# Down projection in 29 blocks that grow from three pairs to eight, each operand tile loaded once

## The chip, the cores and the metric

The kernel runs on one NeuronCore of a Trainium2 chip. The core has five engines that each work through their own queue in order: TensorE (PE, matrix products; its weight loads are listed as PEld), VectorE (DVE), ScalarE (ACT), GpSimd (POOL) and SyncE (SP), which here only issues transfers. Transfers run on 16 DMA engines. The metric is the device time of one execution in microseconds (us), the median of several runs.

## The reference

One layer of a decoder in float32 on 512 tokens of width 2048: RMS norm, one input projection that feeds three token mixers (dilated attention, a convolution module, banded attention with sinks), an output projection with a residual, then a second RMS norm and a gated feed-forward part. What matters here is the last line:

```python
x = x + mix @ w_out[l]
h2 = _rms_norm(x, norm2_g[l])
x = x + (jax.nn.silu(h2 @ w_gate[l]) * (h2 @ w_up[l])) @ w_down[l]
```

The inner width is 5632, that is 44 tiles of 128. The product with `w_down` is called Down; `h2 @ w_gate` and `h2 @ w_up` are called Wide.

## The kernel before, in words

Everything is held transposed: a tile has 128 channels on its partitions and the 512 tokens along it. To keep float32 accuracy on a TensorE that takes rounded operands (fp32r), a weight tile is split into a rounded part (hi, tile `wh`) and the rest (lo, `wl`).

**Seven products.** Wide and Down use a Strassen-Winograd scheme: each matrix is cut in 2 x 2, and seven products of sums of the quarters take the place of eight. The 44 feature tiles are thereby 22 *pairs* (`NP`), pair j being feature tiles j and j + 22; the 16 output tiles are eight pairs n and n + 8. For every pair j there are seven operand tiles, one for each product q, each [128, 512] fp32r (256 KB; first half rounded, second half the rest). Wide computes them, ScalarE and VectorE split them, and they are stored to DRAM (`od[j]`), in four pieces (`sums1` to `piece4`, lines 972 to 1007) whose work stretches over the nine products after the block's last one.

**Blocks.** The last part of the kernel is a loop over blocks (lines 1068 to 1106): 44 Wide blocks, then the Down blocks of the list `DOWN` (d0, d1, ...). A Down block is (n, first, end): it adds to output tiles n and n + 8 what the pairs from first to end - 1 give. Its width w is end - first. Every output pair gets several blocks; between them its two tiles y live in DRAM (`x2d`), are loaded ahead of a block (`load_y`, two transfers, issued in the fourth product of the block before) and stored after it (`store`, four transfers of half a tile). The last block of an output pair stores to the result `outT`.

A block runs the seven products in the order 5, 1, 7, 6, 2, 4, 3 (`ORDER`). For a Down block each product is w matmuls of 512 columns with the rounded weights (L912) and w of 256 columns with the rest (L915). Here d4.3 stands for the fourth product of block d4.

**Weights of a block.** Four tiles of raw weights ("11", "12", "21", "22", each 128 x 128w) are loaded by SP (L209). GpSimd makes the sums that the seven products need (L174), due by product: four products ahead of the block, s = 21 + 22; three ahead, 21 = 21 + 11 in place; at its first product, s = s + 11 in place; at its third, s = s + 12. In the order of the products the weights are s, 11, 21, s, 12, 22, s. Each is split two products ahead of its use (`SPLIT_AHEAD`): ScalarE casts it into PSUM (L226, tile `wn`) and into SBUF (L227, `wh`, three buffers), VectorE subtracts (L228, `wl`, three buffers). There is one buffer each for the raw tiles 11, 12 and 21, two for 22 and two for s; a load for the next block waits until the last split that reads its buffer is done. So the next block's 21, 22 and 11, which are loaded in that order, are issued when the split of the block's third weight is done.

**Evacuation.** After each product the result is added from PSUM on VectorE in the iteration that follows: nothing after the first (it is taken with the third), one reduction after the second (L921), four sums after the third, two after each of the others (L926, L927). After the fourth come three sums of y on GpSimd (L1048 to L1050).

**Operand tiles of Down.** They sit in a pool of 71 tiles of 256 KB. After product i of a block, the tiles of that product which later blocks do not need are given up, and those that the next block needs in addition are loaded (`load_act`, L1064), issued by SP one product later. SP's transfers are issued in the order in which the program names them: one that waits for its buffer or its data holds up all behind it.

**The list before.** 24 blocks, three for each output pair, every one 6, 7 or 8 pairs wide, with a window that slides by one pair a block and wraps:

```
d0..d7    0-6  0-7  1-8  2-9  3-10 4-11 5-12 6-13      (first-end, n = 0..7)
d8..d15   6-14 7-15 8-16 9-17 10-18 11-19 12-20 13-21
d16..d23  14-22 15-22 16-23 17-24 18-25 19-26 20-27 21-28
```

Pairs from 22 on mean 0 to 5 again: these are loaded a second time (28 pairs of seven tiles in all), and a block that wraps loads each of its raw weight tiles in two transfers. d0 needs 42 tiles; they are loaded during the last Wide block, each product's six after that product has been done there.

Of the kernel before, what the change touches and what calls it, by code (L numbers as in the profile page):

```python
# [9 lines left out]
F32 = mybir.dt.float32  # L10
# [5 lines left out]
P = 128  # L16
T = 512
# [7 lines left out]
NF = 44  # L25
# [39 lines left out]
NP = NF // 2  # L65


_A = [0, 0, 1, 2, 3, 4, 5, 6]
_B = [_A[n] + (6 if n == 0 else 7) for n in range(8)]
_C = [b + 8 for b in _B]  # L70
DOWN = [(n, *w) for ab in (zip(_A, _B), zip(_B, _C), zip(_C, [a + NP for a in _A])) for n, w in enumerate(ab)]

LAID = (5, 7, 6, 4, 3, 1, 2)

# [35 lines left out]
def kernel(ctx: ExitStack, tc: tile.TileContext, xT, wi, wo, wgu, wd, cst_in, outT):  # L110
    nc = tc.nc
# [21 lines left out]
    def bank(name, cols=T):  # L133
        return psum["banks"].tile([P, cols], F32, name=name, tag="b")
# [55 lines left out]

    def down_block(n, half, first, end):

        parts = [(first, min(end, NP)), (0, end - NP)] if first < NP else [(first - NP, end - NP)]
        return [bass.AP(tensor=wd.tensor, offset=wd.offset + (n * P * NF + half * NP + a) * P,
                        ap=[[NF * P, P], [1, (b - a) * P]]) for a, b in parts if b > a]

    for t, (n, first, end) in enumerate(DOWN):
        group(f"d{t}", t % 2, (end - first) * P, {f"{i + 1}{k + 1}": down_block(n + 8 * i, k, first, end)
# [3 lines left out]
    at = {"entry": 0, "split": 0, "use": 0}  # L202
# [159 lines left out]
    for k in range(KT):  # L362
# [9 lines left out]
        hi, lo = h_hl.pop(k)  # L372
# [14 lines left out]
    def project(name):  # L387
        b = bank(name)
        for half in range(2):
            wh, wl = next_unit()  # L390
            for kk in range(8):
                k = 8 * half + kk
                s = slice(kk * P, (kk + 1) * P)
                mm3(b, wh[:, s], wl[:, s], h_hi[k], h_lo[k], k == 0, k == KT - 1)
                if kk % 2 == 1:
                    ticks.tick()
        return b
# [356 lines left out]
    for name in PROJ[HEAD4:]:  # L754
        kind, what, j = name[0], name[1], name[2:]
# [3 lines left out]
        b = project(name)  # L759
# [19 lines left out]
    b = box = boxes = shared = None  # L779
# [13 lines left out]
    x2d = {n: tc.dram_tile([P, T], F32, name=f"x2d{n}") for n in range(KT)}  # L793
# [46 lines left out]
    for half in range(2):  # L840
        for i, n in enumerate(OUT_ORDER[half]):
            if half == 1 and i == 2:
                ticks.drain()
                b = None
                open_banks(banks=4, high=2)
            b = bank(f"o{half}_{n}")
# [36 lines left out]
    od = {p: tc.dram_tile([P, 7 * T], F32, name=f"od{p}") for p in range(NP)}  # L883
    evacs, extras = [], []
# [6 lines left out]
    def later(n, fn, *args, queue=evacs):  # L891
        while len(queue) <= n:
            queue.append([])
        queue[n].append((fn, *args))
# [118 lines left out]
    def load_y(t):  # L1013
        if t < len(DOWN):
            for n in (DOWN[t][0], DOWN[t][0] + 8):
                y[t, n] = slot(f"y{t}_{n}")
                nc.sync.dma_start(y[t, n], x2d[n])

    class Down(Block):


        def __init__(self, t):
            super().__init__(f"d{t}", t % 2)
            self.n = DOWN[t][0]
            self.out = outT if t >= 16 else x2d
            self.tail = t == len(DOWN) - 1
            self.y1, self.y2 = y.pop((t, self.n)), y.pop((t, self.n + 8))

# [29 lines left out]
    acts = {}  # L1058

    def load_act(q, pairs):  # L1060
        for j in pairs:
            acts[q, j] = slot(f"a{q}_{j}", F32R)
            at = LAID.index(q)
            nc.sync.dma_start(acts[q, j].bitcast(F32), od[j % NP][:, at * T:(at + 1) * T])  # L1064

    EARLY = 6
    blk = gate = None
    for g in range(2 * NP + len(DOWN)):
        t = g - 2 * NP
        if t < 0:  # L1070
            p, m = divmod(g, 2)
            blk = Wide(p, m, gate if m else None)
            gate = blk if m == 0 else None
        else:
            n, first, end = DOWN[t]
            blk = Down(t)
        early_w = []
        for i, q in enumerate(ORDER):
            sums_now()
            run(evacs)  # L1080
            w = next_unit()
            if g == 0 and i < 2:
                blk.multiply(q, w, [ops[q, j] for j in range(EARLY)], last=False)
                early_w.append((q, w))
                if i == 1:
                    for q, w in early_w:
                        blk.multiply(q, w, [ops[q, j] for j in range(EARLY, NJ)], EARLY)
                    norm2a()
            elif t < 0:
                blk.multiply(q, w, [ops[q, j] for j in range(NJ)])  # L1090
            else:
                blk.multiply(q, w, [acts[q, j] for j in range(first, end)])
            if g == 0 and i == 2:
                norm2b()

            if t == -1:
                for j in range(NJ):
                    ops.pop((q, j))
                later(1, load_act, q, range(*DOWN[0][1:]), queue=extras)
            elif 0 <= t < len(DOWN) - 1:  # L1100
                for j in range(first, DOWN[t + 1][1]):
                    acts.pop((q, j))
                later(1, load_act, q, range(end, DOWN[t + 1][2]), queue=extras)
            if t >= -1 and i == 3:
                load_y(t + 1)
            run(extras)
# [85 lines left out]
```

## Time and profile before

| | |
|---|---|
| median of 3 runs | 1939.97 us (1939.64 to 1940.5) |
| profiled execution | 1939.71 us, of which span from first to last instruction 1937.9 us |
| TensorE busy | 1906.1 us (98%) |
| VectorE, ScalarE, GpSimd busy | 1471.6, 1338.9, 995.0 us |
| DMA queue of SP | 317.51 MB, 48.0% of 16 engines over the span |
| operand tiles of Down (a<-od) | 196 transfers of 256 KB |
| first product of Down | starts at 1489.93 us of the span |
| last product of Down | ends at 1934.1 us |

All times in rows are microseconds from the start of the span unless marked ns. "Busy" counts the time in which an engine executes something; matmuls are pipelined, so the distance from one start to the next is the pace. In a row with a tile such as `w('22', 'd1')` the tile is the raw weight "22" of block d1. A bracket at the end of a row gives the idle time before it and what ended it. The clock is the share of full speed that TensorE was granted.

### The profile page before, as it was taken

How to read it: one execution, taken by the hardware profiler on the slowest of the kernel's cores; microseconds unless marked ns; L12 is line 12 of the kernel's file. 1: busy time of each engine (PE TensorE's matmuls, PEld its weight loads, DVE VectorE, ACT ScalarE, POOL GpSimd, SP SyncE). 2: the span in 40 equal slices, each digit the busy share in tenths (PEclk: the TensorE clock that was granted, in tenths of full speed). 3: DMA queues.
4: the chain of work that ended last, by engine and by line, in shares of the span. 5: the costliest groups of instructions: out<-in, count | busy, mean ns of one | idle time of the engine just before them, and what ended most of it. 6: DMA issues, size and time to landing. Idle time of an engine off the chain costs nothing.

```text
span 1937.9 us, 29292 instructions
## 1 busy us (share of the span) xinstructions
PE 1906.1 (98%) x10332; PEld 1644.0 (85%) x10332; DVE 1471.6 (76%) x2508; ACT 1338.9 (69%) x1782; POOL 995.0 (51%) x640
## 2 busy tenths in 40 slices
PE   8999999999999999999999999999999999999999
PEld 7888888878877888888888888888888788888888
DVE  6789998997468677777777777777777577767776
ACT  6356654553356888888888888888877677777675
POOL 0111011000001787878887878788876666656564
PEclk9999999989999999999999999999999999999999
DMA  7222232223342344444444444344438978777675
GB/s 262 83 97 66 66 94 72 75 81 115 121 133 73 122 167 158 142 158 158 162 149 144 172 147 164 128 184 141 173 125 294 366 274 279 264 241 275 205 270 194
DMA packets 125651, 319.48 MB, mean 165 GB/s; under 512 B 14016, under 2 KB 29504, under 8 KB 125504
## 3 DMA queue, kind: packets, MB, share of 16 engines
q1 hardware_dynamic: 125360, 317.51, 48.0%
q8 instruction: 81, 1.33, 0.3%
q14 instruction: 66, 0.54, 0.1%
q10 hardware_dynamic: 144, 0.10, 0.0%
HBM read 259.09 MB, written 57.15 MB: 163 GB/s over the span
## 4 chain that ended last, share of the span: by engine, by line
PE 69%; DVE 2%; DMA 1%; ACT 1%; issue 0%; DVEq 0%; SPq 0%; ACTq 0%
PE out L912 43%; PE out L915 22%; PE o L246 1%; PE o L245 1%; DMA a<-od 1%; PE o L247 1%; DVE h L802 0%; DMA od<-u21st 0%; DVE xr L826 0%; DVE wl L223 0%; DVE ssum L344 0%; DVE ta L813 0%; ACT sr L343 0%; ACT h L808 0%; DVE wl L228 0%
## 5 line engine op out<-in xcount | busy, mean ns | idle before, releaser
L912 PE MATMUL out<-h,wh 128*128 128x512 f32 x2464 | 619.9, 393 | 5.1 <-DVE h L802 4.1
L912 PEld LDWEIGHTS out<-h,wh 128*128 128x128 f32 x2464 | 444.6, 189 | 85.0 <-DVE h L802 4.4
L915 PEld LDWEIGHTS out<-h,wl 128*128 128x128 f32 x2464 | 337.0, 191 | 24.3
L915 PE MATMUL out<-h,wl 128*128 128x256 f32 x2464 | 344.3, 282 | 0.0
L912 PE MATMUL out<-a,wh 128*128 128x512 f32 x1232 | 318.3, 396 | 5.5 <-DMA a<-od 5.0
L912 PEld LDWEIGHTS out<-a,wh 128*128 128x128 f32 x1232 | 222.2, 190 | 50.4 <-DMA a<-od 8.3
L915 PEld LDWEIGHTS out<-a,wl 128*128 128x128 f32 x1232 | 170.7, 191 | 13.1
L915 PE MATMUL out<-a,wl 128*128 128x256 f32 x1232 | 174.6, 283 | 0.0
L222 ACT CAST wh<-w 128x1024 fp32r<-128x1024 f32 (+1 forms) x93 | 96.8, 1041 | 98.4 <-PE o L246 33.6
L223 DVE TENSOR_TENSOR wl<-w,wh 128x1024 fp32r<-128x1024 f32 (+1 forms) x93 | 112.5, 1210 | 63.4 <-ACT wh L222 63.1
L926 DVE TENSOR_TENSOR y<-y,out 128x256 f32<-128x256 f32 x120 | 50.5, 421 | 67.1 <-PE out L915 64.5
L422 DVE SCALAR_TENSOR_TENSOR y<-bu,cst,y 128x511 f32<-128x511 f32 (+14 forms) x120 | 87.7, 731 | 0.7
L174 POOL TENSOR_TENSOR w('s', 'g0')_5639<-w('21', 'g0')_5403,w('22', 'g0')_5439 128x1024 f32<-128x1024 f32 x1 | 2.4, 2406 | 116.2 <-DMA w('11', 'g0')_5506<-in_wgu 116.2
L927 DVE TENSOR_TENSOR y<-y,out 128x256 f32<-128x256 f32 x120 | 50.5, 421 | 4.1
L246 PE MATMUL o<-ml_c,wh 128*128 128x512 f32 x128 | 51.0, 399 | 2.1 <-DVE ml_c L733 2.1
L245 PE MATMUL cq<-hh,wh 128*128 128x512 f32 x128 | 51.3, 401 | 1.4 <-DVE mix_c L701 1.4
L245 PE MATMUL o<-mh_c,wh 128*128 128x512 f32 x128 | 52.0, 407 | 0.0
L247 PE MATMUL o<-mh_c,wl 128*128 128x512 f32 x128 | 50.8, 397 | 0.0
L247 PE MATMUL cq<-hh,wl 128*128 128x512 f32 x128 | 50.0, 390 | 0.0
L246 PE MATMUL cq<-hl,wh 128*128 128x512 f32 x128 | 49.9, 390 | 0.0
L245 PE MATMUL in<-hh,wh 128*128 128x512 f32 x64 | 26.0, 407 | 5.3 <-ACT wh L222 5.3
L246 PEld LDWEIGHTS o<-ml_c,wh 128*128 128x128 f32 x128 | 24.6, 192 | 7.2 <-DVE ml_c L733 2.8
(3093 smaller groups left out, 4824.3 us busy)
## 6 DMA issues: line engine op xcount, KB each, us to landing
a<-od SPq DMA_DIRECT2D x196, 256.0 KB, 5.4
w<-in_wi SPq DMA_DIRECT2D x59, 512.0 KB, 3.6
w<-in_wo SPq DMA_DIRECT2D x32, 512.0 KB, 3.6
y<-x2d SPq DMA_DIRECT2D x48, 256.0 KB, 5.4
x2d<-y SPq DMA_DIRECT2D x64, 128.0 KB, 3.4
x<-in_xT SPq DMA_DIRECT2D x16, 256.0 KB, 7.2
xr<-in_xT SPq DMA_DIRECT2D x16, 256.0 KB, 3.9
x2d<-xr SPq DMA_DIRECT2D x16, 256.0 KB, 4.0
```

What stands on the lines that cost most here:

```text
L174: nc.gpsimd.tensor_add(out[:, :n], raws[key[a]][0][:, :n], raws[key[b]][0][:, :n])
L222: nc.scalar.copy(hi[:, :n], t[:, :n])
L223: eng.tensor_sub(lo[:, :n], t[:, :n], hi[:, :n].bitcast(F32))
L245: nc.tensor.matmul(out, wh, xh, start=start, stop=False)
L246: nc.tensor.matmul(out, wh, xl, start=False, stop=False)
L247: nc.tensor.matmul(out, wl, xh, start=False, stop=stop)
L422: nc.vector.scalar_tensor_tensor(yconv[j][:, i:], hconv[j][:, :T - i], c, yconv[j][:, i:], op0=ALU.mult, op1=ALU.add)
L912: nc.tensor.matmul(b, wh[:, s], x, start=s.start == 0 and q in (5, 1, 6, 7), stop=False, skip_group_check=True)
L915: nc.tensor.matmul(b[:, TH:], wl[:, s], x[:, :TH], start=False, stop=last and x is xs[-1], skip_group_check=True)
L926: sign(out, out if first is None else first, main)
L927: sign(out, out, rest)
```

## The change

The list `DOWN` is written anew: 29 blocks. Each of the eight output pairs gets three blocks in three rounds, and five of them get a fourth:

```
d0..d7    0-3  0-3  0-4  0-4  0-5  0-6  0-7  0-8       (first-end, n = 0..7)
d8..d15   3-9  3-10 4-11 4-12 5-13 6-14 7-15 8-16
d16..d23  9-16 10-16 11-17 12-18 13-20 14-22 15-22 16-22
d24..d28  16-22 16-22 17-22 20-22 18-22                (n = 0, 1, 2, 4, 3)
```

No range wraps, so every operand tile is loaded once (22 pairs) and every raw weight tile in one transfer. The pair-products are as many as before (176 times seven). d0 needs 21 tiles. `LAST[t]` is the number of pairs loaded for blocks up to t, `FIRST[t]` the first pair that block t or a later one needs; loading and giving up follow these. In d0, d2, d15, d16 and the blocks from d21 on nothing is loaded for a next block; in d19 and d20 two pairs are. `self.out` is chosen by whether a later block has the same n.

```diff
-_A = [0, 0, 1, 2, 3, 4, 5, 6]
-_B = [_A[n] + (6 if n == 0 else 7) for n in range(8)]
-_C = [b + 8 for b in _B]
-DOWN = [(n, *w) for ab in (zip(_A, _B), zip(_B, _C), zip(_C, [a + NP for a in _A])) for n, w in enumerate(ab)]
+ROUNDS = ((3, 3, 4, 4, 5, 6, 7, 8), (9, 10, 11, 12, 13, 14, 15, 16), (16, 16, 17, 18, 20, 22, 22, 22))
+DOWN = [(n, a, b) for lo, hi in zip(((0,) * 8,) + ROUNDS, ROUNDS) for n, (a, b) in enumerate(zip(lo, hi))]
+DOWN += [(n, ROUNDS[-1][n], NP) for n in (0, 1, 2, 4, 3)]
+
+FIRST = [min([w[1] for w in DOWN[t:]] + [NP]) for t in range(len(DOWN) + 1)]
+LAST = [max(w[2] for w in DOWN[:t + 1]) for t in range(len(DOWN))]
...
     def down_block(n, half, first, end):
 
-        parts = [(first, min(end, NP)), (0, end - NP)] if first < NP else [(first - NP, end - NP)]
-        return [bass.AP(tensor=wd.tensor, offset=wd.offset + (n * P * NF + half * NP + a) * P,
-                        ap=[[NF * P, P], [1, (b - a) * P]]) for a, b in parts if b > a]
+        return [bass.AP(tensor=wd.tensor, offset=wd.offset + (n * P * NF + half * NP + first) * P,
+                        ap=[[NF * P, P], [1, (end - first) * P]])]
...
-            self.out = outT if t >= 16 else x2d
+            self.out = x2d if any(w[0] == self.n for w in DOWN[t + 1:]) else outT
...
-            nc.sync.dma_start(acts[q, j].bitcast(F32), od[j % NP][:, at * T:(at + 1) * T])
+            nc.sync.dma_start(acts[q, j].bitcast(F32), od[j][:, at * T:(at + 1) * T])
...
-                for j in range(first, DOWN[t + 1][1]):
+                for j in range(FIRST[t], FIRST[t + 1]):
                     acts.pop((q, j))
-                later(1, load_act, q, range(end, DOWN[t + 1][2]), queue=extras)
+                later(1, load_act, q, range(LAST[t], LAST[t + 1]), queue=extras)
```

## The prediction

> Blocks and products are named as above: d4.3 is the fourth product of block d4, w a block's width in pairs, S(d2) the start of TensorE on d2.
>
> **What bounds the kernel now.** I read the busy time by stretch first, then the chain that ended last, then the timelines of TensorE, of the DMA queue and of VectorE, ScalarE and GpSimd. Two stretches of Down (columns: length, PE, PEld, DVE, ACT, POOL, clock, DMA share, GB/s):
>
> ```profile
> 1489.00:1523.00 34.00, 28.48 (x121) 20.08 (x120) 15.88 (x28) 16.22 (x23) 14.25 (x12) 0.90 1.05 393
> 1523.00:1934.00 411.00, 411.00 (x2354) 361.34 (x2353) 297.48 (x456) 291.62 (x317) 248.11 (x158) 1.00 0.75 259
> ```
>
> In the first 34 us the DMA engines are full and TensorE is not; in the other 411 us TensorE never stops. So all that a new order of blocks can win lies in the first stretch, and how much is read from TensorE's rows:
>
> ```profile
> 1489.93 1.55 PE L912 MATMUL out<-a,wh 128*128 128x512 f32 x6
> ...
> 1523.07 1.78 PE L912 MATMUL out<-a,wh 128*128 128x512 f32 x7
> ...
> 1931.49 1.78 PE L912 MATMUL out<-a,wh 128*128 128x512 f32 x7
> 1933.10 0.99 PE L915 MATMUL out<-a,wl 128*128 128x256 f32 x7
> ```
>
> From d1.2 (1523.07) to d23.6 (1931.49) lie 35 + 156 x 7 + 42 = 1169 pair-products: 408.42 / 1169 = 0.349 us each, of which 0.23 in the 512-column pass and 0.12 in the 256-column one (1.61 us between the last two rows, over 7). Down has 176 x 7 = 1232, or 430.4 us. Begun at 1489.93 it would end at 1920.3; 0.17 us of pipeline tail makes it 1920.5, and the last row ends at 1934.1. **Down loses 13.6 us, all before 1523.** Two causes:
>
> ```profile
> 1485.38 16.83 SPq L1064 DMA_DIRECT2D a<-od  x24
> ...
> w('22', 'd1')_14819<-in_wd SPq DMA_DIRECT2D x1, 448.0 KB, 6.3
> ...
> w('22', 'd2')_15030<-in_wd SPq DMA_DIRECT2D x1, 448.0 KB, 5.1
> ...
> w('21', 'd0')_14549<-in_wd SPq DMA_DIRECT2D x1, 384.0 KB, 3.2
> ```
>
> The queue hands out 24 operand tiles at 0.70 us each, the pace of full DMA engines (256 KB at 393 GB/s is 0.67), and d1's weights stand behind them. The other rows are landing times: 6.3 us in the thick of it, 5.1 as it thins, 3.2 in front of it. Then the clock (columns: length, PE busy, clock, DMA):
>
> ```profile
> 349.00:351.00 2.00, 0.28 (x2) 1.00 0.78 244
> 351.00:355.00 4.00, 3.72 (x13) 0.59 0.00 0
> 542.00:544.00 2.00, 1.22 (x5) 1.00 0.64 252
> 1508.00:1512.00 4.00, 0.89 (x4) 1.00 1.04 389
> 1512.00:1519.00 7.00, 6.82 (x18) 0.52 1.05 400
> ```
>
> After 3.1 idle us of 4 the clock is 0.52 for 7 us, which costs 3.4; after 1.7 idle of 2 it is 0.59 over 4 us, costing about 1.7; 0.8 idle of 2 costs nothing.
>
> **The change, part by part.** *Removed:* 42 of 196 operand loads (28 pairs become 22), 21 of them out of the first stretch, since d0 needs 3 pairs for 6; and the 24 extra weight loads of the blocks that wrapped. In steady state no wait of TensorE hangs on these, so only the 21 count: 21 x 0.67 = 14 us of DMA time. *Added:* five blocks, each with two y loads, four stores, 13 evacuation instructions on VectorE, 14 casts on ScalarE, four weight sums and three y sums on GpSimd. TensorE gets nothing more. Between wide blocks this hides behind products of 2.1 to 2.8 us; it is narrow blocks where the fixed part no longer fits. What a block costs VectorE:
>
> ```profile
> 1904.78 0.69 DVE L921 TENSOR_REDUCE d22u<-out 128x256 f32<-128x512 f32 x1 [1.29 <-PE out L915]
> 1905.38 1.08 DVE L228 TENSOR_TENSOR wl<-w('12', 'd22')_19059,wn 128x896 fp32r<-128x896 f32 x1
> 1907.22 0.42 DVE L926 TENSOR_TENSOR y<-y,out 128x256 f32<-128x256 f32 x1 [0.76 <-PE out L915]
> ...
> 1908.92 1.08 DVE L228 TENSOR_TENSOR wl<-w('22', 'd22')_19005,wn 128x896 fp32r<-128x896 f32 x1
> 1909.92 0.41 DVE L926 TENSOR_TENSOR d22u<-d22u,out 128x256 f32<-128x256 f32 x1
> ...
> 1910.71 1.08 DVE L228 TENSOR_TENSOR wl<-w('s', 'd22')_19078,wn 128x896 fp32r<-128x896 f32 x1
> ```
>
> From start to start: a reduction 0.60, the four sums after the third product 1.70, a pair of sums 0.79 (four a block), together 5.46 us whatever the width; a weight subtraction 1.00 at w = 7. With width it goes as
>
> ```profile
> L228 DVE TENSOR_TENSOR wl<-w('s', 'd12')_17074,wn 128x1024 fp32r<-128x1024 f32 x3 | 3.6, 1217 | 0.8 <-PE out L915 0.8
> ...
> L227 ACT CAST wh<-w('s', 'd12')_17074 128x1024 fp32r<-128x1024 f32 x3 | 3.2, 1052 | 2.3 <-PE out L912 2.3
> ```
>
> 0.13 us a pair (1.217 against 1.08), so 0.5 at w = 3 and 0.35 at w = 2. VectorE needs 5.46 + 7 x 0.5 = 9.0 us for a block of 3 against TensorE's 7.3; 9.8 against 9.8 at w = 4; 7.9 against 4.9 at w = 2. GpSimd and ScalarE, with Wide's leftovers in d0:
>
> ```profile
> 1509.33 2.07 POOL L174 TENSOR_TENSOR w('s', 'd1')_14902<-w('21', 'd1')_14817,w('22', 'd1')_14819 128x896 f32<-128x896 f32 x1 [13.55 <-DMA w('22', 'd1')_14819<-in_wd]
> 1511.48 2.09 POOL L174 TENSOR_TENSOR w('21', 'd1')_14817<-w('21', 'd1')_14817,w('11', 'd1')_14821 128x896 f32<-128x896 f32 x1
> 1513.53 0.72 POOL L1048 TENSOR_TENSOR y<-y,d0u 128x256 f32<-128x256 f32 x1
> ...
> 1516.39 0.73 POOL L983 TENSOR_TENSOR u21tb<-u21tb,u21l 128x256 f32<-128x256 f32 x1
> ```
>
> ```profile
> 1517.15 0.59 ACT L991 CAST u21n<-u21tb 128x512 fp32r<-128x512 f32 x1 [3.94 <-POOL u21tb L983]
> 1518.17 0.62 ACT L992 CAST u21st<-u21tb 128x512 fp32r<-128x512 f32 x1 [0.42 <-DMA od<-u21st]
> 1518.69 0.90 ACT L226 CAST wn<-w('11', 'd1')_14821 128x896 fp32r<-128x896 f32 x1
> 1519.53 0.94 ACT L227 CAST wh<-w('11', 'd1')_14821 128x896 fp32r<-128x896 f32 x1
> ```
>
> This is an order that the change leaves as it is. On GpSimd come d1's first two weight sums, three sums of y, two sums of Wide's last operand (3.6 us for these five); ScalarE holds that operand's casts ahead of d1.1's casts, so d1.1 waits for all of it. A weight sum costs 2.1 ns a column ((2.09 - 0.72) / 640): 1.0 us at w = 3, 1.3 at 4, 1.6 at 5. A cast is 0.94 at 896 columns and 1.05 at 1024, so about 0.45 at w = 3, 0.55 at 4, 0.65 at 5.
>
> *Start of Down, worked forward.* d0 starts at 1489.9 as before; its first products last 1.05 us. The subtraction for d0.2 ends at 1491.4 (sums of the last Wide product 0.8, then 0.5), which frees the buffer for d1's weights: the second tile is issued at 1491.9. Its landing lies between 3.2 and 6.3; the queue has 18 tiles ahead of it instead of 36, so I take 4.3, between the row in front of the crowd and the row behind it: 1496.2. GpSimd: first sum to 1497.3, second to 1498.4, y and Wide's sums 3.6 to 1502.0. ScalarE: Wide's two casts (about 0.52 each from start to start) to 1503.1, d1.1's two to 1504.0. TensorE, through d0 by about 1499 (the last three tiles, issued at 1493, land then) and d1.0 by 1500, idles 4 us. On VectorE, Wide's subtraction (0.6), two evacuation pairs and the subtractions of d1.1 and d1.2 follow the casts: 1503.2 + 1.6 + 1.0 = 1505.8. That frees the buffers for d2: second tile issued at 1506.3, landed 4.4 later (the queue now carries Wide's last stores, y and pair 3) at 1510.7, summed by 1512.0, cast twice by 1513.1. So S(d2) = 1513.2, where an unhindered TensorE would be at 1489.93 + 42 x 0.349 = 1504.6: **8.6 us lost**. With 3.2 in both places it is 6.3, with 6.3 in both 12.5. The half clock that a 4 us gap brings (rows above) slows d1.1 to d1.3 from 1.05 to 2.1 us each, but d1 then ends by about 1512.5, still ahead of d2's weights: cost 0.
>
> d2 and d3 (w = 4, 9.8 us): after the second weight sum (1.3), three y sums (2.1) and the third weight sum (1.3) come two casts (1.1) for the fourth product, which make it late by 0.4 and 0.5. On the DMA queue the store of y waits for the first y sum (about 1514 in d2's place), and the last tiles of pair 3 stand behind it; they are needed from 1519 on: 0. d4's weights: issued 2.7 after S(d3), 5.3 to land (pair 4 beside it), 1.6 for the sum, 1.3 for two casts, 10.9 against 9.8 + 0.5, rounded to **0.8**. Together **1.7** (0, if landings are 3.2, to 3). From d4 on (12.2 us and more) VectorE has 1.5 us and more to spare and the loop through the weight buffers closes in time: nothing.
>
> *End.* d27 (w = 2) lasts 4.9 us. d28's first weight buffer is free 1.4 after S(d27), its second tile is issued at 1.9, lands at 5.5 (no operand is loaded any more; 3.2 and its place behind the first), sum 1.3, casts 1.2: S(d28) = S(d27) + 8.1 instead of 4.9. **Lost 3.2**, and **0.4** where d28.3 waits for the third sum. Bounds 2.8 and 5. VectorE, with 7.9 us, stays just within the same 8.1. TensorE stands still for 1.8 us before d28 and 1.4 in bits before that. For the clock the nearest row is the 1.7 idle us at 349, so I count 1.7 less the 0.4 already waited: **1.3**; bounds 0 and 3.4.
>
> The Trainium skill, TensorE: Matmul & The Clock Gate, section "Why this matters for your kernels", would let gaps below about 3 us pass without a lower clock; the row at 349 says otherwise. By the rule the sum would be 1.3 us smaller, 1940.3.
>
> The sum: 8.6 + 1.7 + 3.6 + 1.3 = 15.2 lost for 13.6: **1.6 us more**. The profiled execution took 1939.71 (span 1937.9 and 1.8 around it), 0.26 under the median of the runs: 1941.3 as profiled, 1941.6 as a median, +0.08%.
>
> **Rivals.** *A, faster: the queue is nearly empty once half the operand tiles are gone.* All landings at 3.2: start 6.3, d2 to d4 0, end 2.8, clock 0: 9.1 lost, 4.5 less than now: **1935.5**. For it: 14 us of DMA time less. Against it: Wide's stores, y and d0's and d1's weights remain, and VectorE alone needs some 10.5 us for d0 with Wide's leftovers. It decides from landings below about 3.5 us.
>
> *B, slower: the queue stays full through d4.* A block of 3 that loads a pair moves 0.8 MB of weights, 1.05 of y in and out, 1.84 of operands, 3.7 MB in 7.3 us where 393 GB/s carry 2.9; d3 moves 4.2 MB in 9.8 us (3.8). Then landings are 6.3: start 12.5, d2 to d4 3.0, the rest as forecast: 20.4 lost: **1946.8**. Against it: d0 and d2 load no pair, and the stalls give the queue time. From landings of about 5.3 on it counts as slower.
>
> *C, no effect:* d0's wait only moves to d1, and the narrow blocks cost as much as they save: **1940.0**.
>
> **How the numbers follow.** The measurement can tell about 0.2% (3.9 us) from no change. Forecast 0.45, A 0.2, B 0.27, C 0.08. A and B reach beyond the bounds 1936.1 and 1943.9; the forecast's own range, 1937 to 1944.5, and C lie almost wholly between: faster 0.2, same 0.5, slower 0.3. The range takes in A and B: 1934.5 to 1948.
>
> **What would show it.** TensorE: d0 without the waits for operand tiles of before, an idle stretch of 3 to 5 us ended by ScalarE's casts after d1.0, a clock near 0.5 behind it; small waits in d2 to d4; no waits from d5 to d26; one of 1.5 to 2.5 us before d28. GpSimd: the first sum of d1 at about 1496 instead of 1509. Wrong if no gap stands after d1.0 (then A), if blocks d2 to d4 begin late by more than 1 us each (B), or if TensorE waits between d5 and d26.

## The result, and the profile after

The changed kernel takes 1944.54 us (median of 11 runs, 1943.32 to 1945.35), the kernel before 1939.68 beside it (11 runs, 1938.88 to 1940.5): ratio 1.0024, 95% interval 1.0016 to 1.0032. The forecast was 1941.6 with a range of 1934.5 to 1948. The time lies in the range, 2.9 us above the forecast and at the upper end of the forecast's own range (1944.5). The ratio is just past the forecast's 0.2% line, which lies inside the interval; taken as it stands, of the three outcomes it is "slower", to which 0.3 was given, and not "the same", to which 0.5 was given.

First the busy time by stretch of the changed kernel (columns: length, PE, PEld, DVE, ACT, POOL, clock, DMA share, GB/s), the same two stretches as before:

```profile
1489.00:1523.00 34.00, 29.08 (x138) 22.96 (x136) 27.21 (x60) 20.86 (x44) 19.56 (x21) 0.90 0.91 319
1523.00:1934.00 411.00, 406.55 (x2302) 354.49 (x2303) 309.56 (x512) 294.27 (x363) 256.81 (x182) 1.00 0.73 251
```

The first stretch is better than it was (29.08 busy us instead of 28.48, DMA engines 0.91 instead of 1.05), though by little. The second, where TensorE never stopped before, now has 4.5 idle us. TensorE's timeline shows where (start, length, tile, count, and in brackets the idle time before it with what ended it):

```profile
1489.09 0.86 PE L913 MATMUL out<-a,wh 128*128 128x512 f32 x3
...
1497.32 2.07 PE L913 MATMUL out<-a,wh 128*128 128x512 f32 x3 [1.45 <-DMA a<-od]
...
1499.83 1.45 PE L913 MATMUL out<-a,wh 128*128 128x512 f32 x3
...
1503.83 1.07 PE L913 MATMUL out<-a,wh 128*128 128x512 f32 x3 [2.19 <-ACT wh L228]
...
1512.07 1.20 PE L913 MATMUL out<-a,wh 128*128 128x512 f32 x4
...
1524.33 1.19 PE L913 MATMUL out<-a,wh 128*128 128x512 f32 x4 [0.30 <-ACT wh L228]
...
1535.70 1.43 PE L913 MATMUL out<-a,wh 128*128 128x512 f32 x5 [0.50 <-ACT wh L228]
...
1549.05 0.50 PE L913 MATMUL out<-a,wh 128*128 128x512 f32 x1 [1.26 <-DMA a<-od]
...
1549.98 1.54 PE L913 MATMUL out<-a,wh 128*128 128x512 f32 x6
...
1919.67 0.63 PE L913 MATMUL out<-a,wh 128*128 128x512 f32 x2
...
1927.20 1.60 PE L913 MATMUL out<-a,wh 128*128 128x512 f32 x4 [1.09 <-ACT wh L228]
...
1938.21 0.63 PE L916 MATMUL out<-a,wl 128*128 128x256 f32 x4
```

The rows without a bracket at 1489.09, 1499.83, 1512.07 and 1919.67 are the starts of d0, d1, d2 and d27; 1524.33, 1535.70, 1549.98 and 1927.20 those of d3, d4, d5 and d28. The bracket names only the last bit of a stall; what a block loses is its length from start to start less 7 w pair-products of 0.3494 us (the forecast's unit to one more digit). So d2 lasts 12.26 us and needs 28 x 0.3494 = 9.78: it loses 2.48.

| | before | after | forecast for after |
|---|---|---|---|
| d0, d1 | 11.72 + 1.87 | 3.40 + 4.90 = 8.3 | 8.6 |
| d2, d3, d4 | 0 | 2.48 + 1.59 + 2.05 = 6.1 | 1.7 |
| d5 to d26 | 0 | 0.21 in d5, 0.2 in all the others | 0 |
| d27, up to the start of d28 | 0 | 2.64 | 3.2 |
| d28 | 0 | 1.69 | 0.4 + 1.3 |
| sum | 13.5 | 19.1 | 15.2 |

That is 5.6 us more lost. Down began 0.84 us earlier in this execution (1489.09 against 1489.93; the same code up to there gave 1488.65 and 1490.08 in two experiments, so this is spread), and the stretch behind TensorE's last row is 0.1 longer: 5.6 - 0.84 + 0.1 = 4.9, the difference of the spans, 1942.8 against 1937.9. One term carries it: **d2 to d4, 6.1 us where 1.7 was forecast.**

The loop that makes most of these 6.1 us is seen when the other engines are read beside TensorE. Issues of d3's first two weight tiles on SP's queue, the first weight sum of d3 on GpSimd, and VectorE's evacuation in d2, all of the changed kernel:

```profile
1512.34 0.75 POOL L1049 TENSOR_TENSOR y<-y,d1u 128x256 f32<-128x256 f32 x1
1513.04 0.76 POOL L1050 TENSOR_TENSOR y<-y,d1u 128x256 f32<-128x256 f32 x1
...
1521.82 1.29 POOL L176 TENSOR_TENSOR w('s', 'd3')_15122<-w('21', 'd3')_15072,w('22', 'd3')_15074 128x512 f32<-128x512 f32 x1 [3.09 <-DMA w('22', 'd3')_15074<-in_wd]
```

```profile
1513.82 0.42 DVE L927 TENSOR_TENSOR y<-y,out 128x256 f32<-128x256 f32 x1 [1.43 <-POOL y L1050]
...
1516.01 0.68 DVE L229 TENSOR_TENSOR wl<-w('21', 'd2')_14932,wn 128x512 fp32r<-128x512 f32 x1
```

```profile
1516.75 0.38 SPq L210 DMA_DIRECT2D w('21', 'd3')_15072<-in_wd  x1
1517.18 0.42 SPq L210 DMA_DIRECT2D w('22', 'd3')_15074<-in_wd  x1
```

Read from the top. GpSimd does the two weight sums of d2 and only then, from 1512.34, d1's three sums of y. VectorE has to add d1's sixth product to a y tile that these sums write, and waits 1.43 us for them. Behind that wait on VectorE stands the third weight subtraction of d2, which is the last reader of the raw tile 21 (1516.01 to 1516.69). At 1516.75 SP issues d3's tile 21, at 1517.18 its tile 22: 5.1 us after the start of d2. They land 4.5 us later, and GpSimd, idle for 3.09 us, begins the next round at 1521.82. The circle closes: weights land, weight sums, sums of y, VectorE's evacuation, third subtraction, buffer free, weights issued. In d3 and d4 VectorE waits 1.46 and 1.48 us for the sums of y, and the second tile is issued 4.9 and 5.2 us after the block's start (1529.21 and 1540.90).

SP issues in order, so the late weights hold up operand tiles too. The last tile of pair 3 is issued right behind d3's weights, the last of pair 4 right behind d5's, and TensorE waits for them in the last products of d2 (0.39 us) and d4 (1.26 us). By themselves they cost little, since ScalarE's casts for the next block end late as well. SP's issues of the two tiles, and ScalarE's cast for d5's first product:

```profile
1518.17 0.38 SPq L1065 DMA_DIRECT2D a<-od  x1
...
1542.72 0.38 SPq L1065 DMA_DIRECT2D a<-od  x1
```

```profile
1548.72 0.83 ACT L228 CAST wh<-w('s', 'd5')_15418 128x768 fp32r<-128x768 f32 x1
```

That cast ends at 1549.55, so without the wait for the tile d5 could have begun 0.4 us earlier at most; d3's start, at 1524.33, follows ScalarE's cast and not the tile.

### The profile page after: what moved, and what is told of

The parts are those of the page before. It is cut to its first block, busy times and chain, and to the rows that moved or that the text cites. A ratio compares the mean times of both kernels' runs of the same rounds, so it can differ in the third digit from the quotient of the medians.

```text
span 1942.8 us, 29614 instructions
## 1 busy us (share of the span) xinstructions
PE 1907.3 (98%) x10332; PEld 1644.8 (85%) x10332; DVE 1498.5 (77%) x2608; ACT 1346.1 (69%) x1852; POOL 1008.7 (52%) x675
## 3 DMA queue, kind: packets, MB, share of 16 engines
q8 instruction: 81, 1.33, 0.3%
## 5 line engine op out<-in xcount | busy, mean ns | idle before, releaser
L913 PE MATMUL out<-a,wh 128*128 128x512 f32 x1232 | 323.0, 397 | 7.5 <-ACT wh L228 4.1
L916 PEld LDWEIGHTS out<-a,wl 128*128 128x128 f32 x1232 | 175.9, 192 | 20.8 <-DVE wl L229 4.3
L916 PE MATMUL out<-a,wl 128*128 128x256 f32 x1232 | 181.5, 284 | 1.9 <-DVE wl L229 1.6
L927 DVE TENSOR_TENSOR y<-y,out 128x256 f32<-128x256 f32 x145 | 60.9, 420 | 59.1 <-PE out L916 42.7
L928 DVE TENSOR_TENSOR y<-y,out 128x256 f32<-128x256 f32 x145 | 61.1, 421 | 5.0
```

Of the source, the lines that this page charges most:

```text
L913: nc.tensor.matmul(b, wh[:, s], x, start=s.start == 0 and q in (5, 1, 6, 7), stop=False, skip_group_check=True)
L916: nc.tensor.matmul(b[:, TH:], wl[:, s], x[:, :TH], start=False, stop=last and x is xs[-1], skip_group_check=True)
L927: sign(out, out if first is None else first, main)
L928: sign(out, out, rest)
```

## The experiments

Losses of TensorE are counted as in the table above, each from one profiled execution; the interval of a ratio is about 0.1% to either side. Each ratio is against the kernel before on the same chip.

### Which part of the loop: the order on GpSimd

The first try was to break the circle at GpSimd: let the sums of y go ahead of the next block's first two weight sums.

```diff
-        sums[u - 4].append(add("s", "21", "22"))
+        sums[u - (3 if name[0] == "d" and name != "d0" else 4)].append(add("s", "21", "22"))
...
         for i, q in enumerate(ORDER):
-            sums_now()
+            if t < 0 or i != 4:
+                sums_now()
```

> The changed kernel, but on GpSimd the three sums of y of each Down block go ahead of the next block's first two weight sums instead of behind them. Loop theory: VectorE's evacuation of the last two products waits for these sums of y, they wait behind the weight sums, those wait for the weights, and the next weights wait for a subtraction behind that evacuation. With the order turned, the subtraction that frees the raw weights of d3 ends about 2 us after the start of d2 instead of 4.6, and the 6.1 us lost in d2, d3 and d4 shrink to about 1.5; d28's wait shrinks little, since its weights are issued early already. Time about 1940 (4 to 5 us less than the changed kernel's 1944.5). Rival, a full DMA queue: the landings set these losses, the order on GpSimd does not matter, time 1943.5 to 1944.5.

Measured: 1974.47 us, ratio 1.0182 (1.0168 to 1.0196). A clear miss: Down loses 49.0 us, and most blocks lose. GpSimd around the start of d3, and then SP and TensorE, in this kernel:

```profile
1526.95 0.74 POOL L1049 TENSOR_TENSOR y<-y,d2u 128x256 f32<-128x256 f32 x1 [5.19 <-PE out L916]
...
1529.04 1.26 POOL L176 TENSOR_TENSOR w('s', 'd3')_15149<-w('21', 'd3')_15072,w('22', 'd3')_15074 128x512 f32<-128x512 f32 x1
```

```profile
1519.58 0.33 SPq L210 DMA_DIRECT2D w('21', 'd3')_15072<-in_wd  x1
```

```profile
1531.52 1.33 PE L913 MATMUL out<-a,wh 128*128 128x512 f32 x4 [2.31 <-ACT wh L228]
```

The weights of d3 are issued at 1519.58, but GpSimd stands idle for 5.19 us before the sums of y, because these need the fourth product, and the weight sums behind them begin at 1529.04. What I had read as "the sums of y are late" is only half of it: they cannot be early either, since their input comes from TensorE late in the block. One link of the loop is borne out all the same. With the sums of y first, VectorE does not wait for them at the start of d2 (1516.62 in this kernel), and its third subtraction ends 2.9 us after that start, for 4.6 in the changed kernel:

```profile
1518.83 0.68 DVE L229 TENSOR_TENSOR wl<-w('21', 'd2')_14932,wn 128x512 fp32r<-128x512 f32 x1
```

So neither order on GpSimd is free of a wait in a narrow block. What the run does show is that a wait put ahead of GpSimd's weight sums goes straight into TensorE's time.

### Which part of the loop: the transfers

The rival for d2 to d4 was full DMA engines. Here pairs 3, 4 and 5 are not loaded at all; the products of these pairs take the tiles of pair 0, so their true share is left out of the result.

```diff
         for j in pairs:
+            if j in (3, 4, 5):
+                acts[q, j] = acts[q, 0]
+                continue
```

> The changed kernel without the loads of the operand tiles of pairs 3, 4 and 5: their products use pair 0's tiles, so the output is wrong in that part; products, weights and everything else stay. It takes 5.5 MB out of the DMA queue in d1, d3 and d4. Rival, a full DMA queue: of the 6.1 us lost in d2 to d4 hardly any stays (at most 1), time about 1939.5. Loop theory: the weights land in about 3.0 us instead of 3.4 to 5.2, but d2 and d3 stay at 10.5 us or more against 9.8, and only d4's wait for operand tiles (1.3) goes altogether: about 2.5 of the 6.1 stay, time about 1941.

Measured: 1942.27 us, ratio 1.0014 (1.0005 to 1.0023). d2, d3 and d4 lose 1.36 + 1.87 + 0.53 = 3.8 us of 6.1, although the second weight tile of d3 now lands in 3.1 us (4.5 with the loads). With 21 transfers gone, 3.8 us stay, and d5 loses 0.63 for 0.21; the other 2.3 us hang on these transfers, by contention or by tiles that come late, which this run does not separate. This is between the two expectations (2.5 and at most 1), and rather beyond the one of the loop: lighter traffic alone does not end it.

### The loop cut open: a second buffer for raw tile 21

With two buffers for 21, the load no longer waits for the third subtraction. The buffer takes the place of two of the 71 slots.

```diff
-N_SLOTS = 71
+N_SLOTS = 69
-RAW_PLAIN = "22b sb 21 22a 11 sa 12".split()
+RAW_PLAIN = "22b sb 21a 22a 11 sa 12".split()
...
-            entries.append((k + "ab"[m] if k == "22" else k, key[k], blocks[k]))
+            entries.append((k + "ab"[m if name[0] == "d" or k == "22" else 0] if k[0] == "2" else k, key[k], blocks[k]))
...
-        pump(RAW_EARLY if u < 20 else RAW_BUFS)
+        pump(RAW_EARLY if u < 20 else RAW_BUFS + 1)
```

> The changed kernel with a second buffer for the raw weight tile 21 of Down's blocks (and 69 operand slots for 71, to make room). The weights of a block are then issued about a block earlier and no longer wait for the third subtraction of the block before. Loop theory (landing, weight sums, y sums, evacuation, subtraction, next issue): the loop is open, d2, d3 and d4 lose at most 0.5 us each plus what operand tiles are late (together 2 or less, instead of 6.1), d2 starts about 1 us earlier, and d28 is held only by VectorE's surplus (about 1.5 instead of 2.6, with no half clock behind it). Time 1936.5 to 1938.5, below the kernel before. Rival, the time is set by full DMA engines: the same bytes move, d2 to d4 lose 5 or more, time 1943 to 1944.5.

Measured: 1940.79 us, ratio 1.0008 (1.0000 to 1.0017). SP's queue, TensorE at the start of d2 and in its third product, and GpSimd in this kernel:

```profile
1510.43 0.43 SPq L210 DMA_DIRECT2D w('21', 'd3')_14975<-in_wd  x1
```

```profile
1514.13 1.09 PE L913 MATMUL out<-a,wh 128*128 128x512 f32 x4
...
1519.07 0.50 PE L913 MATMUL out<-a,wh 128*128 128x512 f32 x1 [1.27 <-DMA a<-od]
```

```profile
1519.43 1.29 POOL L176 TENSOR_TENSOR w('s', 'd3')_15124<-w('21', 'd3')_14975,w('22', 'd3')_14998 128x512 f32<-128x512 f32 x1
```

d3's tile 21 is issued 3.7 us before d2 begins, instead of 4.7 after. The first weight sum of d3 stands 5.3 us after the start of d2 instead of 9.75, though the second tile takes 4.1 us to land, hardly less than the 4.5 of the changed kernel. d2 to d4 lose 1.58 + 0 + 0.37 = 1.95 us instead of 6.1, and 1.27 of that is one operand tile. d27 and d28 gain too, 1.39 + 0.26 for 2.64 + 1.69. Down loses 11.34 us, 7.8 less. **The moment at which the buffer comes free, and not the time to land, made most of the loss in d2 to d4.** The time fell only by half of the 7.8 us and missed the 1936.5 to 1938.5 expected: Down began 2.8 us later, at 1491.93, and the stretch behind TensorE's last row grew by 0.6.

Are those 2.8 us the price of the two slots? The changed kernel with 69 slots and nothing else:

```diff
-N_SLOTS = 71
+N_SLOTS = 69
```

> The changed kernel with 69 operand slots instead of 71 and nothing else. Every theory: no effect, 1944.5 within 1 us; a block holds at most 8 pairs of seven tiles and loads one more by and by.

Measured: 1947.58 us, ratio 1.0043 (1.0028 to 1.0058; three executions). I had expected nothing, and it costs 3 us: Down begins at 1492.04, 2.95 us late, while Down itself loses 18.0 us, no more than before. The busy time of TensorE from 0 to 1489 falls from 1466.86 to 1463.88 us, and from 500 on the two do not differ (981.97 us each up to 1489): the slots are short in the first 500 us, far from the change. One of the stretches that lost, in the changed kernel and then with 69 slots (columns: length, PE, PEld, DVE, ACT, POOL, clock, DMA share, GB/s):

```profile
350.00:360.00 10.00, 9.31 (x44) 8.05 (x45) 9.54 (x20) 2.35 (x4) 1.51 (x1) 0.83 0.20 68
```

```profile
350.00:360.00 10.00, 7.84 (x34) 6.15 (x33) 9.76 (x19) 3.56 (x6) 0.00 (x0) 0.83 0.18 57
```

### The start: the sums of Wide's last operand two products earlier

```diff
-                    for n, piece in ((0, self.sums1), (1, self.piece3), (3, self.piece1), (4, self.sums2),
+                    for n, piece in ((0, self.sums1), (1, self.piece3), (3, self.piece1), (2 if self.p == NP - 1 else 4, self.sums2),
```

> The changed kernel, but GpSimd makes the two sums of the last Wide block's last operand in d0's third product instead of its fifth, ahead of d1's weight sums. Theory that ScalarE, held by that operand's casts, makes the gap after d1.0: the wait of 2.2 us there goes, d1.1 starts at about 1501.5 instead of 1503.8, one stretch of half clock goes, d2's weights are issued some 3 us earlier and d2 starts 2.5 to 3.4 us earlier (1508.7 to 1509.5). Time about 1941.5. Rival, DMA: d2's weights then meet Wide's stores in the queue and land as late as before; d2 starts at 1511 or later, time 1943.5 to 1944.5.

Measured: 1942.61 us, ratio 1.0016 (1.0007 to 1.0025). d2 begins 20.5 us after d0 instead of 23.0, and d0 and d1 lose 1.99 + 3.80 = 5.8 us for 8.3: the 2.5 us expected. So these 2.5 us of the forecast's first term were made where it was said to be, in GpSimd's row of sums ahead of ScalarE's casts for d1.1; the other 5.8 were not taken apart. The time fell by 1.9 us, not by the 3 expected. What is left of the gap (1.33 us before d1.1) has moved on: the second of Wide's two casts on ScalarE now waits 1.45 us for the store of an earlier piece out of the same staging buffer.

### The end: the narrow block last

```diff
-DOWN += [(n, ROUNDS[-1][n], NP) for n in (0, 1, 2, 4, 3)]
+DOWN += [(n, ROUNDS[-1][n], NP) for n in (0, 1, 2, 3, 4)]
```

> The changed kernel, with its last two blocks exchanged: the block of four pairs (n = 3) comes before the block of two pairs (n = 4). If the 2.6 us before d28 and the half clock behind it (1.7) come from d28's weights, which a block of 4.9 us is too short to bring in, both go: a block of 9.8 us precedes now, and what is left is VectorE's surplus in the last block, 7.9 against 4.9 us less two products of lead, about 1.7. Time about 1942 (2.5 less than 1944.5). Rival, VectorE's fixed work in the block of two pairs is the cause: the loss stays at about 4, time 1944 to 1945.

Measured: 1943.23 us, ratio 1.0020 (1.0011 to 1.0029). d27, now four pairs wide, loses nothing, and d28 with two pairs 1.61: 1.6 us left of 4.3, close to what was expected. But the end behind TensorE grows from 3.9 to 5.15 us (the span of 1942.0 less TensorE's last end at 1936.85), which takes 1.2 of it back. GpSimd and VectorE at the very end of this kernel:

```profile
1937.46 0.72 POOL L1051 TENSOR_TENSOR y<-y,d28u 128x256 f32<-128x256 f32 x1
```

```profile
1937.54 0.42 DVE L927 TENSOR_TENSOR y<-y,out 128x256 f32<-128x256 f32 x1 [0.46 <-POOL y L1050]
...
1938.78 0.42 DVE L928 TENSOR_TENSOR y<-y,out 128x256 f32<-128x256 f32 x1
```

In a block of two pairs the sums of y are not done when the sixth product is, so VectorE's last evacuations run behind them, after TensorE has finished.

### Put together

Second buffer for 21 (69 slots), early sums and narrow block last in one kernel; its edits are the three above.

> Three edits at once: the second buffer for tile 21, the two sums of Wide's last operand in d0's third product, and the last two blocks exchanged. If the three losses (gap after d1.0, loop in d2 to d4, the short block at the end) are separate, the gains add up: another 2 us for Wide's sums and 1 for the exchange beside the second buffer alone, time 1934 to 1936, faster than both kernels. Rival, one loss is only handed to the next: no better than the second buffer alone.

Measured: 1940.48 us, ratio 1.0003 (0.9994 to 1.0012): 4 us better than the change, but 4.5 to 6.5 short of what I expected. The slots cost their 2.9 us again (Down begins at 1491.98), the tail its 1.2, and the gap before d1.1 is still 2.0 us. ScalarE in this kernel shows who holds it now:

```profile
1503.73 0.62 ACT L993 CAST u21st<-u21tb 128x512 fp32r<-128x512 f32 x1 [2.82 <-DMA od<-u21st]
```

That is the wait for the staging buffer again, twice as long; a store of Wide's now stands on SP (1498.07) behind weights of d2 that are issued earlier.

Is the narrow start as such the fault? The same kernel with the first round's ranges ending at 5, 5, 5, 5, 5, 6, 7 and 8 instead of 3, 3, 4, 4, 5, 6, 7 and 8:

```diff
-ROUNDS = ((3, 3, 4, 4, 5, 6, 7, 8),
+ROUNDS = ((5, 5, 5, 5, 5, 6, 7, 8),
```

> The three edits, and the first round begins with five pairs (5 5 5 5 5 6 7 8) instead of three (3 3 4 4 5 6 7 8); the second and third rounds end where they did, so the blocks behind are narrower by as much. d0 then needs 35 operand tiles instead of 21, 14 x 0.67 = 9 us more of DMA time before its last product. Theory that the narrow start is right once weights are early: slower than with the three edits alone by 3 us or more. Rival, narrow blocks cost by their fixed work on VectorE whatever the buffers: faster than with the three edits alone.

Measured: 1941.51 us, ratio 1.0011 (1.0002 to 1.0020). d0 loses 6.9 us instead of 2.7, d1 to d4 2.4 instead of 6.0: Down's losses differ by 0.8 us. It is slower by 1 us, not by the 3 and more that I expected. Between these two kernels, five pairs or three to begin with makes almost no difference; what d0 waits longer for its operand tiles, d1 to d4 wait less for weights.

Now the second buffer without loss of slots: where a block has at most four pairs, its tile 21 fits into one ordinary slot, and only d1, d3 and d27 take it. Beside it the store piece of Wide's last operand stands two products later. Early sums, the narrow block last and the edits of `RAW_PLAIN` and `pump` stay as above; not shown again.

```diff
-            entries.append((k + "ab"[m] if k == "22" else k, key[k], blocks[k]))
+            two = m if k == "22" or name[0] == "d" and n <= T else 0
+            entries.append((k + "ab"[two] if k[0] == "2" else k, key[k], blocks[k]))
...
-        raws[key] = (wp.tile([P, 1024], F32, name=f"w{key}", tag=f"raw{buf}", bufs=1), n)
+        raws[key] = (slot(f"w{key}") if buf == "21b" else
+                     wp.tile([P, 1024], F32, name=f"w{key}", tag=f"raw{buf}", bufs=1), n)
...
-                                     (5, self.piece2), (8, self.piece4)):
+                                     (7 if self.p == NP - 1 else 5, self.piece2), (8, self.piece4)):
```

> All 71 slots again; the second raw buffer of tile 21 is one of them, taken only by odd blocks of at most four pairs (d1, d3, d27); Wide's n2/n4 sums two steps early, the last blocks 3 and 4 exchanged, and the store piece of u21tb two steps later (behind the casts of d1.2). Theory of the loop over GpSimd and of the slots: Down starts at 1489-1490 again (1491.98 with 69 slots), the gap before d1.1 falls from 2.0 us to below 1, and Down loses 8 to 10 us instead of 19.1: 1935 to 1937.5, faster than both kernels. Rival (landings and the full DMA queue set the start of d1 to d4): the gap stays near 2 us or moves behind d1.1, losses 11 or more: 1939 to 1941.

> As the run beside it, but with the store piece of u21tb at its old step. If that piece's wait for its stage buffer is what holds d1.1, the gap of 2.0 us stays here and this kernel is 1 to 2 us slower than the run beside it, 1937 to 1938.5; if something else holds d1.1 the two agree within 0.5 us. Against the run with 69 slots (1940.5) the slots alone are worth about 2.9 us.

Measured: 1938.60 us with the piece moved, ratio 0.9995 (0.9986 to 1.0004), and 1938.69 without, 0.9997 (0.9988 to 1.0005). Down begins at 1489.62 and 1490.17, so the slots' 2.9 us are back; by the two ratios (0.9997 against 1.0003) the time is 1.2 us less than with 69 slots, but the two intervals overlap. With the piece moved no gap is left before d1.1 (waits of at most 0.5 us stand inside d1); without, it is 1.98 us. That is as expected, yet the medians agree: in the profiles the two differ by 1.5 us in Down's losses (10.6 and 12.1), but the runs of the second spread from 1936.2 to 1942.4, and 1.5 us of one execution is within that. Whether moving the piece helps stays open. Both are a little worse than expected because of a wait in d2. TensorE in d2.2 and SP's queue, with the piece moved:

```profile
1514.82 0.50 PE L915 MATMUL out<-a,wh 128*128 128x512 f32 x1 [1.96 <-DMA a<-od]
...
1515.83 1.91 PE L915 MATMUL out<-a,wh 128*128 128x512 f32 x4
```

```profile
1507.41 0.33 SPq L212 DMA_DIRECT2D w('22', 'd3')_14998<-in_wd  x1
1507.84 0.92 SPq L1020 DMA_DIRECT2D y<-x2d  x2
1508.85 0.92 SPq L1067 DMA_DIRECT2D a<-od  x2
```

The operand tile that d2.2 needs is issued at 1508.85, behind d3's weights and y. Two ways to issue it earlier, both with the last blocks in the change's own order again. First, two tiles instead of one at each product of d1 and d3:

```diff
-                later(1, load_act, q, range(LAST[t], LAST[t + 1]), queue=extras)
+                for k in ORDER[2 * i:2 * i + 2] if t < 4 else (q,):
+                    later(1, load_act, k, range(LAST[t], LAST[t + 1]), queue=extras)
```

> The run with 71 slots and the early sums, but with the last blocks in the change's own order (two pairs, then four) and the operand tiles of pairs 3 to 5 issued two at each product instead of one. If the wait of 1.96 us at d2.2 came from the place of that load in the order of the queue, d2 loses under 1 us (3.85 there); the end, with the second buffer of tile 21, loses 1.7 ahead of the last row and 0.5 behind it, against 1.6 and 1.2 with the narrow block last. Together 2 us less: 1936 to 1937, faster than the kernel before by 0.15%. If full DMA engines set that landing, d2 loses as much as before: 1938 to 1939.

Second, pair 3 loaded in d0 already:

```diff
 LAST = [max(w[2] for w in DOWN[:t + 1]) for t in range(len(DOWN))]
+LAST[1] = 4
```

> As the run beside it, but with one operand tile at each product, and pair 3's seven tiles issued in d0 instead of d1. By the order on the queue the wait in d2 goes wholly. By full DMA engines the 4.7 us of transfers come back in the landings of d1's and d2's weights: d0 and d1, 4.8 us in the run with 71 slots, lose 1 to 3 us more and the time is 1937 to 1939; without contention 1936 to 1936.5.

Measured: 1938.21 us, ratio 0.9993 (0.9984 to 1.0002), and 1939.06 us, ratio 0.9995 (0.9986 to 1.0004). In the first, d2 loses 1.08 us for 3.85, so the place in the queue was the cause of that wait; but d3 and d4 now lose 1.31 and 0.78 where they lost nothing, Down's losses are 10.6 us as before, and the 1936 to 1937 expected were missed. TensorE, in d3 of the first kernel and in d1 of the second:

```profile
1524.84 0.74 PE L918 MATMUL out<-a,wl 128*128 128x256 f32 x4 [1.02 <-DVE wl L231]
```

```profile
1505.47 0.96 PE L916 MATMUL out<-a,wh 128*128 128x512 f32 x3 [1.25 <-ACT wh L231]
...
1509.81 1.65 PE L916 MATMUL out<-a,wh 128*128 128x512 f32 x3 [3.03 <-ACT wh L231]
```

In the second, d2 and d3 lose almost nothing, but d0 and d1 lose 2.96 + 6.99 = 9.95 us for 4.8: seven transfers moved ahead by one block cost 5.1 us there, more than the 1 to 3 I had expected from contention. In these two runs whatever was issued earlier at the start of Down was paid for by something else that came later.

The lowest median is that of the kernel with two tiles at each product: 0.3% faster than the change (0.9993 against 1.0024), but not to be told from the three others in which an ordinary slot is the second buffer, nor from the kernel before, since its interval reaches to 1.0002.

## Why the prediction was right or wrong

**The balance of the first stretch: right, its size partly by luck.** d0 and d1 lose 8.3 us; 8.6 was forecast. The chain of waits was the one described. The first weight sum of d1, forecast at 1496.2, and ScalarE's cast for Wide, forecast at 1502.0, in the changed kernel:

```profile
1496.15 1.00 POOL L176 TENSOR_TENSOR w('s', 'd1')_14838<-w('21', 'd1')_14781,w('22', 'd1')_14783 128x384 f32<-128x384 f32 x1 [2.05 <-DMA w('22', 'd1')_14783<-in_wd]
```

```profile
1501.82 0.59 ACT L992 CAST u21n<-u21tb 128x512 fp32r<-128x512 f32 x1 [3.71 <-POOL u21tb L984]
...
1511.40 0.61 ACT L228 CAST wh<-w('s', 'd2')_14984 128x512 fp32r<-128x512 f32 x1
```

d1.1 was forecast for 1504.0 and began at 1503.83; d2's second weight tile was forecast to be issued at 1506.3 and was at 1506.38. It landed in 3.0 us instead of the 4.4 assumed, which is why d2 begins at 1512.07 and not at 1513.2. But Down began 0.84 us early: counted from its start, the links up to that issue came 0.6 to 0.9 us late (d1's second tile took 4.9 us to land, not 4.3), and the short landing of d2's tile made up for it. The gap before d1.1 is 2.19 us, not 4, because d1.0 ended at 1501.6, not at 1500: behind d0's wait of 1.45 us for an operand tile the clock was halved, which the forecast did not have, and d0's last product and d1.0 took 2.51 and 1.81 us instead of 1.05 each. The half clock behind the gap was costed at 0, since d1 would end before d2's weights are there; it did, but only just: d1's last product, begun at 1510.73 and 1.05 long, ends at 1511.8, d2's cast at 1512.0.

**d2 to d4: wrong, and this is the failed step.** "Together 1.7 (0, if landings are 3.2, to 3)" measured 6.1, twice the upper bound. Inside it the step that failed is the time of issue: "d4's weights: issued 2.7 after S(d3)". It was 4.9, with 5.1 in d2 and 5.2 in d4. The cause is a wait that I had left out. I let the three sums of y delay GpSimd's third weight sum and the store on SP, but not VectorE, which needs them for its next evacuations and has the third subtraction behind these in its queue. In d3 that wait is 1.46 us of the 2.2 by which the issue came late; the rest was not broken down. The landing was taken too long for it (5.3; measured 3.4 for d4's second tile), so the two errors partly cancel in d3 (forecast start of d4 10.9 after d3, measured 11.37), and not in d2 and d4, for which no loop was worked out at all. "From d4 on ... the loop through the weight buffers closes in time: nothing" was wrong for d4 (2.05) and right from d6 on; in d5 it is 0.21. The second buffer for 21, which cuts just this loop, took 4.2 of the 6.1 us away.

**The last tiles of pair 3 behind the store of y, "0": wrong in kind.** The last products of d2 and d4 waited 0.39 and 1.26 us for a tile that stood on SP behind the next block's weights, not behind the store of y. These waits lie for the most part beside those for the weights. The run without the loads of pairs 3 to 5 shows 2.3 us for late tiles and contention together. Where the loop had been cut, the order of issue was worth 2.8 us in d2 (3.85 to 1.08), but gave nothing in sum.

**The end: right.** Up to the start of d28 2.64 us (3.2), in d28 1.69 (0.4 + 1.3). The clock term can be read off. TensorE in four stretches of the changed kernel (length, PE busy, clock, DMA share, GB/s):

```profile
1498.00:1501.00 3.00, 3.00 (x8) 0.50 1.01 389
...
1549.00:1553.00 4.00, 3.95 (x22) 1.00 1.05 396
...
1926.00:1928.00 2.00, 0.91 (x4) 0.95 0.76 276
1928.00:1931.00 3.00, 3.00 (x10) 0.50 0.38 127
```

The wait for d28's weights (1.1 idle us of 2) is followed by 3 us at half clock, 1.5 us lost; so is the 1.45 us wait in d0. The Trainium skill, TensorE: Matmul & The Clock Gate, section "Why this matters for your kernels", warns of gaps above about 3 us only. This trace does not agree: gaps of 1.5 us, and of 1.1 us with smaller ones ahead of it, were enough. The forecast had followed the row and not the rule, and that was worth its 1.3 us, with some luck: not every such gap lowers the clock. Behind the wait of 1.26 us that ends at 1549.05 it stayed at 1.00, and in the kernel of three edits even behind the 2.0 us before d1.1:

```profile
1503.00:1505.00 2.00, 0.23 (x2) 1.00 1.04 406
1505.00:1509.00 4.00, 3.77 (x20) 1.00 0.99 342
```

The length of a gap of 1 to 2 us does not tell, then, whether half clock follows; what does, these runs do not show.

**The rivals.** The times to land decide on A and B. Transfers of the second weight tiles of the changed kernel, size and time from issue to landing:

```profile
w('22', 'd4')_15212<-in_wd SPq DMA_DIRECT2D x1, 320.0 KB, 3.4
...
w('22', 'd2')_14934<-in_wd SPq DMA_DIRECT2D x1, 256.0 KB, 3.0
...
w('22', 'd3')_15074<-in_wd SPq DMA_DIRECT2D x1, 256.0 KB, 4.5
...
w('22', 'd1')_14783<-in_wd SPq DMA_DIRECT2D x1, 192.0 KB, 4.9
```

A (an almost empty queue) is out: d1's second tile took 4.9 us, d3's 4.5, and where a landing was short (3.4 us, d4's tile) the block that waited, d3, still lost 1.59. C (no effect) is out by the interval. B, the full queue through d4, had as its sign that blocks d2 to d4 begin late by more than 1 us each; that sign came (2.48, 1.59, 2.05), but not by B's mechanism. Landings of d2's to d4's second tiles were 3.0 to 4.5 us, never B's 6.3; with the loads taken out 3.8 us stayed; and with the buffer doubled most of the loss went although the tiles landed no faster (5.5, 4.1 and 4.1 us). A sign that two mechanisms share does not tell them apart; the time of issue, which only one of them moves, does.

**Signs that were off.** The idle stretch after d1.0 was 2.19 us, not 3 to 5, and the wait before d28 1.09, not 1.5 to 2.5.

**d6 to d26:** no wait of TensorE there, as forecast. The five further blocks cost nothing where the blocks are wide.

## What to carry to other kernels

When blocks get smaller, follow every buffer's full circle (who frees it, behind what that instruction stands on its own engine, and what that in turn waits for) and give each link a time relative to the block's start; an engine's sum of busy time, which still fitted here, says nothing of it. If a circle is too long, one more buffer at the right place can be worth more than fewer transfers (4.2 us against 2.3 here), but look at what the buffer displaces: two slots taken from a pool cost 2.9 us a thousand microseconds earlier, where the buffer made of them saved 7.8. And check a loss at the end of a program behind the last product as well: what is moved off TensorE may come back in the tail.

## What was not expected of the hardware

Two things. Idle gaps of 1.1 us, with smaller gaps ahead of it, and of 1.45 us were followed by half the clock over the next 3 us, while gaps of 1.26 and 2.0 us were not, as shown above. And a transfer's time to land says little about whether it is late: the second weight tiles of d2 to d4 landed in 3.0 to 4.5 us in the changed kernel and in 4.1 to 5.5 with the second buffer, where TensorE lost a third as much in these blocks.
